# New places in memory for the split weights and the split activations of a float32r decoder trunk

## The chip, the cores and the metric

The kernel runs on one core of a Trainium2 chip. Its time is device time in microseconds (us); two runs of the kernel before gave 2322.8 and 2322.99 us, median 2322.89 us. One more execution was recorded by the hardware profiler, and every row quoted below comes from such a recording.

The core has several engines with instruction queues of their own. PE (TensorE) multiplies matrices; the profile shows its weight loads as a row of their own, PEld, because they run beside the multiplication. DVE (VectorE) and ACT (ScalarE) work elementwise, POOL (GpSimd) does a little copying, and SP (SyncE) issues the weight transfers from HBM.

## The reference

A two-layer decoder trunk over 272 tokens (16 learned meta tokens and 256 input tokens), model width 2048, 16 heads of 128, feed-forward width 8192, all in float32:

```
h = concat(meta, x)                                   # 272 x 2048
a = rms_norm(h);  q,k,v,f = a @ fox_w_in              # layer 0
h += forgetting_attention(q, k, v, cumsum(log_sigmoid(f + b))) @ fox_w_o
h += square(relu(rms_norm(h) @ w_up[0])) @ w_down[0]
c = rms_norm(h);  K,V = c @ w_kv                      # shared K/V
h += stick_breaking_attention(rms_norm(h) @ sb_w_q, K, V) @ sb_w_o   # layer 1
h += square(relu(rms_norm(h) @ w_up[1])) @ w_down[1]
return rms_norm(h)[16:]
```

The weight products are nearly all of the work. Layer 0 and the shared K/V need all 272 tokens; from the query projection of layer 1 on, only the last 256 tokens are needed.

## The kernel before, in words

**Split numbers.** Each float32 operand of a large product is split into a high part (the number rounded to float32r, the reduced format that PE takes in one pass) and a low part (the rest). Of the four partial products three are kept: high weight times high activation, high weight times low activation, low weight times high activation. ACT writes the high parts (line 217 for weights, line 134 for activations), DVE writes the low parts (lines 218 and 135). Activations that come out of attention are split by `put_split` (line 358), and those of the feed-forward layer at lines 503 and 504.

**Groups.** `gemm_group` (line 182) computes 512 output features, in four accumulators `acc` of 128 features each (index m). It goes through 2048 input features in four blocks (kb) of four chunks of 128 (kc). A weight block is brought in by SP in two transfers of 512 KB (line 204), and each half is split into a tile `whi` and a tile `wlo` (lines 209 and 210). A half holds two chunks, so a tile is 2 x 512 numbers per partition. There are four buffers for each of `raw`, `whi` and `wlo`. The groups are numbered by a counter u from 1 to 96, in this order: 1 to 12 the projections of layer 0 (q, k, v for four heads at a time, attention work between them), 13 to 16 its output projection, 17 to 48 its feed-forward layer (four rounds of four up groups and four down groups), 49 to 52 the queries of layer 1, 53 to 60 the shared K and V with the attention of layer 1 between them, 61 to 64 the output projection, 65 to 96 the feed-forward layer of layer 1.

**Two forms of the inner loop.** A group over 272 tokens issues, for each chunk and each m, three matmuls with 272 moving columns (lines 247 to 249), 192 in a group. A group over 256 tokens is "paired": the high and the low part of a row of activations stand side by side, so that one matmul with 512 moving columns multiplies the high weight with both (line 237), and a second one with 256 columns multiplies the low weight with the high part (line 241); that is 64 matmuls of either kind in a group. The two halves of the accumulator are added up when it is emptied (lines 254 and 258). Group 96 takes its last accumulator in the form of three. Every matmul loads its own weights.

**Places.** A tile of split activations has room for 16 rows of 640 numbers and 64 more. `ROWS` (line 28) gives, for 272 tokens, a row pitch of 640 numbers, the high part at number 48 and the low part at 368; for 256 tokens a pitch of 576, the high part at 16 and the low part at 272. In the allocated program the tiles `whi`, `wlo` and `x` all start at multiples of 256 bytes. So, counted in bytes past a multiple of 256, weights start at 0 (a chunk is 2048 bytes and a block of 128 features 512 bytes); activation rows for 272 tokens start at 192, high and low alike, and those for 256 tokens at 64, high and low alike.

**What sets the order.** The Python order of the calls, arranged by the tile framework's own scheduler, fixes each engine's instruction order; within the groups the matmuls are tied to their written order (line 174). PE takes its instructions in that order.

**Other float32r matmuls.** The forget-gate products (lines 305 and 306) multiply the same activation rows of 272 with weight tiles that are 32 features wide; those tiles start at 32 and at 160 bytes past a multiple of 256. In the attention of layer 1, lines 600 to 605 multiply tiles of two runs of 256 or 144 columns, whose first number stands 224 bytes past a multiple of 256, with weights at 32.

Of the kernel before, what the change touches and what calls it, by code (L numbers as in the profile page):

```python
# [10 lines left out]
F32R = mybir.dt.float32r  # L11
# [4 lines left out]
P = 128  # L16
D = 2048
NC = D // P
M = 16
# [4 lines left out]
QSCALE = 1.0 / math.sqrt(P)  # L24
N_FF = 4


ROWS = {0: (640, 48, 368), M: (576, 16, 272)}
XROW = 640

G_A0, G_M0, G_KV, G_A1, G_M1, G_FIN = range(6)
# [3 lines left out]
def yoco_kernel(ctx: ExitStack, tc: tile.TileContext, hT_in, gains, b_f, w_f, w_qkv0, w_o0, w_up, w_dn,  # L35
# [7 lines left out]
    wspl = ctx.enter_context(tc.tile_pool(name="wspl", bufs=4))  # L43
# [75 lines left out]
    class Split:  # L119


        def __init__(self, label, t0):
            n = T - t0
            self.t0 = t0
            rows = xs.tile([P, NC * XROW + 64], F32R, tag="x", name=f"x_{label}")
            pitch, hi, lo = ROWS[t0]
            rows = rows[:, hi:hi + NC * pitch].rearrange("p (c t) -> p c t", c=NC)
            self.hi, self.lo = rows[:, :, :n], rows[:, :, lo - hi:lo - hi + n]
            self.both = rows[:, :, :2 * n]

    def split_chunk(sp, gi, c):

# [41 lines left out]
    def gemm_matmul(*args, **kw):  # L174

        ins = nc.tensor.matmul(*args, **kw).ins  # L176
        if queued and pinned[0]:
            tc.add_manual_dep(ins, queued[0].name, mybir.DependencyInfo(mybir.DependencyClass.NoSync,
                                                                        mybir.DependencyReason.DATA))
        queued[:] = [ins]  # L180

    def gemm_group(wblk, sp, t0, evac, before={}, after={}, load_x=None, pairs=False, apart=()):

        uid[0] += 1
        u = uid[0]
        accs = [pacc.tile([P, 512], F32, tag="acc", name=f"acc_{u}_{m}") for m in range(4)]  # L190
        n = T - t0
        for kb in range(4):
            src_w = wblk[kb].rearrange("p (k c) -> p k c", k=4)
            if kb in before:
                before[kb]()
            piece = 1 if load_x is not None and kb < 2 else 2
            raws = [wraw.tile([P, 2, 512], F32, tag="raw", name=f"raw_{u}_{kb}_{hf}") for hf in range(2)]
            for k0 in range(0, 4, piece):
                if load_x is not None:
                    load_x(range(4 * kb + k0, 4 * kb + k0 + piece))  # L200
                if load_x is not None and kb == k0 == 0:

                    for c0 in (0, 256):
                        nc.scalar.dma_start(raws[0][:, 0, c0:c0 + 256], src_w[:, 0, c0:c0 + 256])
                else:
                    nc.sync.dma_start(raws[k0 // 2][:, k0 % 2:k0 % 2 + piece], src_w[:, k0:k0 + piece])
            parts = []
            for hf in range(2):
                whi = wspl.tile([P, 2, 512], F32R, tag="whi", name=f"whi_{u}_{kb}_{hf}")
                wlo = wspl.tile([P, 2, 512], F32R, tag="wlo", name=f"wlo_{u}_{kb}_{hf}")  # L210
                boxes = [(o, piece, 0, 512) for o in range(0, 2, piece)]
                if load_x is not None and kb == hf == 0:
                    boxes[:1] = [(0, 1, 0, 256), (0, 1, 256, 512)]
                for o, no, c0, c1 in boxes:
                    src = raws[hf][:, o:o + no, c0:c1]
                    hp, lp = whi[:, o:o + no, c0:c1], wlo[:, o:o + no, c0:c1]
                    on_act = nc.scalar.activation(hp, src, AF.Copy)  # L217
                    on_dve = nc.vector.tensor_tensor(out=lp, in0=src, in1=hp.bitcast(F32), op=ALU.subtract)  # L218
                parts.append((whi, wlo))
            if kb in after:  # L220
                with tc.issue_after(on_act.ins), tc.issue_after(on_dve.ins):
                    after[kb]()


            if load_x is not None and kb == 0:
                runs = [([kc], range(4)) for kc in range(4)]
            elif kb in (0, 3):
                runs = [(range(4), [m]) for m in range(4)]
            else:
                runs = [(range(2 * hf, 2 * hf + 2), range(4)) for hf in range(2)]  # L230
            pinned[0] = load_x is None
            for kcs, ms in runs:
                paired = [m for m in ms if pairs and m not in apart]
                single = [m for m in ms if m not in paired]
                for kc in kcs:
                    for m in paired:
                        gemm_matmul(accs[m], parts[kc // 2][0][:, kc % 2, m * P:(m + 1) * P], sp.both[:, 4 * kb + kc],
                                    start=kb == kc == 0, stop=False)
                for kc in kcs:
                    for m in paired:  # L240
                        gemm_matmul(accs[m][:, :n], parts[kc // 2][1][:, kc % 2, m * P:(m + 1) * P],
                                    sp.hi[:, 4 * kb + kc], start=False, stop=kb == kc == 3)
                for m in single:
                    for kc in kcs:
                        wh, wl = (w[:, kc % 2, m * P:(m + 1) * P] for w in parts[kc // 2])
                        hi, lo = sp.hi[:, 4 * kb + kc], sp.lo[:, 4 * kb + kc]
                        gemm_matmul(accs[m][:, :n], wh, hi, start=kb == kc == 0, stop=False)
                        gemm_matmul(accs[m][:, :n], wh, lo, start=False, stop=False)
                        gemm_matmul(accs[m][:, :n], wl, hi, start=False, stop=kb == kc == 3)
                if kb == 3:  # L250
                    for m in ms:
                        evac(m, [accs[m][:, :n]] + ([accs[m][:, n:]] if m in paired else []))
# [18 lines left out]
    def load_x(chunks):  # L271
        c0, n = chunks[0], len(chunks)
        nc.sync.dma_start(hT[:, c0:c0 + n, :], hT_in[:, c0:c0 + n, :])
        if c0 == 0:
            nc.sync.dma_start(g_sb, gains)
        for c in chunks:
            split_chunk(xa, G_A0, c)
# [86 lines left out]
    for g in range(4):  # L364
# [11 lines left out]
        if g == 0:  # L376

            gemm_group(w_qkv0[0], xa, 0, lambda m, acc, qT=qT: nc.scalar.copy(qT[:, m, :], acc[0]),
                       after={kb: (lambda kb=kb: first_norm(kb)) for kb in range(4)}, load_x=load_x)
            gate_products()  # L380
            box["rstd"] = norm.finish()
            for m in range(4):
                evac_q(m, [qT[:, m, :]])
            forget_gates(box["rstd"])
        else:
            gemm_group(w_qkv0[3 * g], xa, 0, evac_q)
# [4 lines left out]
        def decays(j):  # L391

            for i, (o, n) in enumerate(((0, 144), (144, T))):
                nc.vector.scalar_tensor_tensor(out=s[:, j, o:o + n], in0=fk[:, j, :n],
                                               scalar=fq_sb[:, i, 4 * g + j:4 * g + j + 1],
                                               in1=maskA[:, o:o + n], op0=ALU.subtract, op1=ALU.add)

        gemm_group(w_qkv0[3 * g + 1], xa, 0, lambda m, acc: evac_kv(m, acc, kT),
                   after={j: (lambda j=j: decays(j)) for j in range(4)})

# [255 lines left out]
    a, y, t, rs = (fin[:, i, :] for i in range(4))  # L656
# [81 lines left out]
```

## Time and profile before

| what | value |
|---|---|
| median of two runs | 2322.89 us |
| profiled execution | 2323.63 us |
| span of its instructions | 2321.9 us |
| PE busy | 2310.8 us (100%) |
| PEld busy | 2190.4 us (94%) |
| DVE busy | 1350.6 us (58%) |
| ACT busy | 1064.0 us (46%) |
| mean granted TensorE clock | 0.998 |

The span runs from the first to the last instruction; the profiled execution is 1.7 us longer than that. Matmuls are pipelined: the duration of one matmul in the profile (some 287 ns for 272 columns) overlaps with the next ones, so the price of a matmul is the distance from its start to the start of the next, which is read from a stretch of known length with a known count of matmuls in it, or from the start times in a timeline.

### The profile page before, as it was taken

What the parts mean: (1) busy time and instruction counts of PE and PEld (TensorE: products, weight loads), DVE (VectorE), ACT (ScalarE), POOL (GpSimd) and SP (SyncE); (2) the same over time, 40 slices, a digit from 0 to 9 for tenths busy, and PEclk for the clock granted to TensorE, in tenths of its full rate; (3) what the DMA queues carried; (4) which work ended last, traced back from release to release, by engine and by line L of the source; (5) the groups of instructions that cost most, each with busy time, mean ns of one, the idle gap of its engine ahead of it and who ended that gap; (6) DMA issues with size and microseconds to landing.
All of it is one profiled execution on the core that took longest, in us unless ns stands there. A gap on an engine that the chain in (4) does not pass through costs nothing.

```text
span 2321.9 us, 39954 instructions
## 1 busy us (share of the span) xinstructions
PE 2310.8 (100%) x16486; PEld 2190.4 (94%) x16486; DVE 1350.6 (58%) x1923; ACT 1064.0 (46%) x1477; POOL 39.9 (2%) x58
## 2 busy tenths in 40 slices
PE   9999999999999999999999999999999999999998
PEld 9999999999999999999998999988888888888887
DVE  7665555655455455445566655567665665665665
ACT  6434344544344344344455444455544543543553
POOL 1000000000000000000000000000000000000000
PEclk9999999999999999999999999999999999999999
DMA  6544444455555455555556444455555555556553
GB/s 233 172 156 165 171 158 173 171 183 173 183 175 183 171 186 176 178 182 171 187 173 200 155 145 146 146 175 186 197 184 193 192 186 198 186 184 199 181 199 127
DMA packets 116630, 412.00 MB, mean 177 GB/s; under 512 B 13264, under 2 KB 16736, under 8 KB 116448
## 3 DMA queue, kind: packets, MB, share of 16 engines
q1 hardware_dynamic: 114560, 406.29, 51.4%
q10 hardware_dynamic: 1888, 3.16, 0.4%
q8 instruction: 129, 2.11, 0.4%
q14 instruction: 53, 0.43, 0.1%
HBM read 407.29 MB, written 2.11 MB: 176 GB/s over the span
## 4 chain that ended last, share of the span: by engine, by line
PE 99%; DMA 0%; DVE 0%; ACT 0%; issue 0%; DVEq 0%; SPq 0%; ACTq 0%
PE acc L176 95%; PE ps L406 0%; PE pza L585 0%; PE pv L339 0%; PE po L468 0%; PE po L624 0%; DMA raw<-w_qkv 0%; PE po L625 0%; PE pzb L586 0%; PE po L469 0%; DMA hT<-hT_in 0%; PE po L626 0%; DVE ob L680 0%; PE pf L306 0%; PE pf L305 0%; PE pta L600 0%
## 5 line engine op out<-in xcount | busy, mean ns | idle before, releaser
L218 DVE TENSOR_TENSOR wlo<-raw,whi 128x1024 fp32r<-128x1024 f32 (+1 forms) x773 | 931.5, 1217 | 746.8 <-ACT whi L217 745.2
L217 ACT ACTIVATE whi<-raw 128x1024 fp32r<-128x1024 f32 (+1 forms) x773 | 799.2, 1050 | 953.9 <-PE acc L176 877.4
L176 PE MATMUL acc<-x_u,whi 128*128 128x272 f32 (+2 forms) x3088 | 647.5, 321 | 0.0
L176 PE MATMUL acc<-x_m,whi 128*128 128x272 f32 (+1 forms) x3072 | 646.1, 322 | 0.0
L176 PEld LDWEIGHTS acc<-x_u,whi 128*128 128x128 f32 x3088 | 499.9, 188 | 26.7
L176 PEld LDWEIGHTS acc<-x_m,whi 128*128 128x128 f32 x3072 | 497.8, 188 | 27.4
L176 PE MATMUL acc<-x_u,wlo 128*128 128x272 f32 (+1 forms) x2048 | 445.9, 282 | 0.0
L176 PE MATMUL acc<-x_m,wlo 128*128 128x272 f32 (+1 forms) x2048 | 443.7, 282 | 0.0
L176 PE MATMUL acc<-x_a,whi 128*128 128x272 f32 (+1 forms) x1792 | 360.6, 306 | 0.4 <-ACT x_a L134 0.2
L176 PEld LDWEIGHTS acc<-x_u,wlo 128*128 128x128 f32 x2048 | 340.3, 188 | 15.7
L176 PEld LDWEIGHTS acc<-x_m,wlo 128*128 128x128 f32 x2048 | 339.5, 188 | 15.9
L176 PEld LDWEIGHTS acc<-x_a,whi 128*128 128x128 f32 x1792 | 284.4, 188 | 9.9 <-issue 0.7
L176 PE MATMUL acc<-x_a,wlo 128*128 128x272 f32 (+1 forms) x1024 | 254.5, 286 | 0.0
L176 PE MATMUL acc<-x_kv,whi 128*128 128x272 f32 x1024 | 194.1, 288 | 0.0
L176 PEld LDWEIGHTS acc<-x_a,wlo 128*128 128x128 f32 x1024 | 179.6, 188 | 4.9 <-issue 0.5
L176 PE MATMUL acc<-x_o,whi 128*128 128x272 f32 (+1 forms) x768 | 162.3, 322 | 0.0
L176 PEld LDWEIGHTS acc<-x_kv,whi 128*128 128x128 f32 x1024 | 160.6, 188 | 0.4
L176 PE MATMUL acc<-x_kv,wlo 128*128 128x272 f32 x512 | 147.3, 288 | 0.0
L256 DVE TENSOR_TENSOR hT<-acc,hT 128x256 f32<-128x256 f32 (+1 forms) x239 | 102.4, 428 | 71.4 <-PE acc L176 69.5
L176 PEld LDWEIGHTS acc<-x_o,whi 128*128 128x128 f32 x768 | 124.3, 188 | 6.8
L176 PE MATMUL acc<-x_o,wlo 128*128 128x272 f32 (+1 forms) x512 | 111.6, 283 | 0.0
L176 PEld LDWEIGHTS acc<-x_kv,wlo 128*128 128x128 f32 x512 | 96.5, 188 | 0.1
(226 smaller groups left out, 1040.0 us busy)
## 6 DMA issues: line engine op xcount, KB each, us to landing
raw<-w_up SPq DMA_DIRECT2D x256, 512.0 KB, 4.7
raw<-w_dn SPq DMA_DIRECT2D x256, 512.0 KB, 4.7
raw<-w_qkv SPq DMA_DIRECT2D x92, 512.0 KB, 3.8
raw<-w_o SPq DMA_DIRECT2D x64, 512.0 KB, 4.5
raw<-w_kv SPq DMA_DIRECT2D x64, 512.0 KB, 3.6
raw<-w_q SPq DMA_DIRECT2D x32, 512.0 KB, 4.6
fk<-f_dram ACTq DMA_DIRECT2D x4, 544.0 KB, 5.0
raw<-w_qkv SPq DMA_DIRECT2D x7, 256.0 KB, 4.8
```

Of the source, the lines that this page charges most:

```text
L176: ins = nc.tensor.matmul(*args, **kw).ins
L217: on_act = nc.scalar.activation(hp, src, AF.Copy)
L218: on_dve = nc.vector.tensor_tensor(out=lp, in0=src, in1=hp.bitcast(F32), op=ALU.subtract)
L256: nc.vector.tensor_tensor(out=hT[:, c, t0:], in0=a, in1=hT[:, c, t0:], op=ALU.add)
```

## The change

The tiles `whi` and `wlo` are allocated 64 numbers wider per chunk (pitch 576 instead of 512 numbers) and used from a first column that a new function gives, separately for the high and for the low weights, by the group's number u: 0, 16, 32 or 48 numbers, which is 0, 64, 128 or 192 bytes. In the up groups of both feed-forward layers the 16 combinations of high and low displacement occur once each; in the down groups the high displacement is 16 or 0 numbers and the low one goes through all four.

The rows of activations have a pitch of 640 numbers in every stage, and each stage has a place for the high and for the low part. In most stages the two parts now stand at different bytes past a multiple of 256: 192 and 0 (`a0`), 0 and 192 (`kv`, `u1_3`), 192 and 64 (`o0`), 0 and 64 (`a1`), 64 and 128 (`o1`), 192 and 0 (`m1`), 128 and 192 (`u1_2`). In the others both stand alike: 192 (`m0`, as before), 224, 240, 160 and 0 (`u0_0` to `u0_3`), 64 and 0 (`u1_0`, `u1_1`).

In paired groups the matmul with 512 columns now reads two runs of 256 columns a given distance apart, 304 numbers in five stages; in `u1_0` and `u1_1` the distance is 256 and the two runs touch, as before. Where the low part stands first in the row, the products of high activations land in the second half of the accumulator, and the matmul of the low weight adds there.

The instructions on every engine and their order are the same as before; the splitting of a full half of weights now writes two runs of 512 numbers instead of one of 1024.

```diff
-ROWS = {0: (640, 48, 368), M: (576, 16, 272)}
+ROWS = {"a0": (48, 384), "kv": (0, 304), "o0": (48, 336), "m0": (48, 368), "u0_0": (56, 376),
+        "u0_1": (60, 380), "u0_2": (40, 360), "u0_3": (0, 320),
+        "a1": (320, 16), "o1": (336, 32), "m1": (304, 0), "u1_0": (16, 272), "u1_1": (0, 256),
+        "u1_2": (352, 48), "u1_3": (0, 304)}
+
+
+def columns_of_weights(u):
+
+    quarter = (0, 16, 32, 48)
+    if u <= 16 or 53 <= u <= 60:
+        return quarter[u % 4], quarter[u % 4]
+    if 49 <= u <= 52 or 61 <= u <= 64:
+        return ((0, 0), (0, 32), (32, 0), (16, 16))[u % 4]
+    f, g = divmod((u - 17) % 48, 8)
+    if g < 4:
+        return quarter[f], quarter[g]
+    return (16 if u < 37 else 0), quarter[g - 4]
...
-            pitch, hi, lo = ROWS[t0]
-            rows = rows[:, hi:hi + NC * pitch].rearrange("p (c t) -> p c t", c=NC)
-            self.hi, self.lo = rows[:, :, :n], rows[:, :, lo - hi:lo - hi + n]
-            self.both = rows[:, :, :2 * n]
+            hi, lo = ROWS[label]
+            o = min(hi, lo)
+            rows = rows[:, o:o + NC * XROW].rearrange("p (c t) -> p c t", c=NC)
+            self.hi, self.lo = (rows[:, :, k - o:k - o + n] for k in (hi, lo))
+
+            d = abs(lo - hi)
+            if t0:
+                self.both = rows[:, :, :2 * d].rearrange("p c (i t) -> p c i t", i=2)[:, :, :, :n]
+            self.low_first = lo < hi
...
-                whi = wspl.tile([P, 2, 512], F32R, tag="whi", name=f"whi_{u}_{kb}_{hf}")
-                wlo = wspl.tile([P, 2, 512], F32R, tag="wlo", name=f"wlo_{u}_{kb}_{hf}")
+                whi, wlo = (wspl.tile([P, 2, 576], F32R, tag=f"w{x}", name=f"w{x}_{u}_{kb}_{hf}")[:, :, o:o + 512]
+                            for x, o in zip(("hi", "lo"), columns_of_weights(u)))
...
-                        gemm_matmul(accs[m][:, :n], parts[kc // 2][1][:, kc % 2, m * P:(m + 1) * P],
+                        gemm_matmul(accs[m][:, n:] if sp.low_first else accs[m][:, :n],
+                                    parts[kc // 2][1][:, kc % 2, m * P:(m + 1) * P],
```

## The prediction

> **What bounds the kernel now.** I read the first page of the profile first (busy shares, the chain that ended last), then the stretches of one stage each with the matmuls of line 176 alone, then the timeline of PE for single start times.
>
> ```profile
> span 2321.9 us, 39954 instructions
> PE 2310.8 (100%) x16486; PEld 2190.4 (94%) x16486; DVE 1350.6 (58%) x1923; ACT 1064.0 (46%) x1477; POOL 39.9 (2%) x58
> PE 99%; DMA 0%; DVE 0%; ACT 0%; issue 0%; DVEq 0%; SPq 0%; ACTq 0%
> core 0: 2321.9 us, clock 0.998
> ```
>
> The chain of work that ended last is PE for 99% of the span, at a granted clock of 0.998. PE has practically no idle time, so only two things can change the time: how many matmuls there are, and how far apart they start. To price a matmul I take two stretches in which nothing but group matmuls run, four groups each: down groups over 272 tokens, then down groups over 256 tokens (columns: stretch, its length, PE busy and count, PEld busy and count, granted clock, DMA).
>
> ```profile
> core 0: us, PE busy (x) PEld busy (x), PEclk, DMA share, GB/s
> 525.20:619.90 94.70, 94.70 (x770) 94.70 (x769) 1.00 0.53 178
> 1687.60:1776.10 88.50, 88.50 (x513) 77.72 (x512) 1.00 0.58 190
> ```
>
> Four groups over 272 tokens are 4 x 192 = 768 matmuls (the other two of the 770 belong to the neighbours): 94.70 us / 768 = **123.3 ns** each. Four paired groups are 256 pairs of a 512-column and a 256-column matmul: 88.50 us / 256 = **345.7 ns** a pair. The kernel has 56 groups of the first form and 40 of the second: 56 x 192 x 123.3 ns = 1326 us and 40 x 64 x 345.7 ns = 885 us, together 2211 us, 95% of the span. The other 111 us are attention, norms and the two ends, which the change does not touch.
>
> Is there room in these prices that could hang on a place in memory? The timeline of PE in a paired group says so (columns: start, length, engine and line, operation, count; a row begins where the one before it has issued its last matmul).
>
> ```profile
> 1709.74 1.09 PE L176 MATMUL acc<-x_u,whi 128*128 128x512 f32 x4
> 1710.67 0.62 PE L176 MATMUL acc<-x_u,wlo 128*128 128x256 f32 x4
> 1711.12 1.07 PE L176 MATMUL acc<-x_u,whi 128*128 128x512 f32 x4
> 1712.03 0.63 PE L176 MATMUL acc<-x_u,wlo 128*128 128x256 f32 x4
> 1712.50 0.40 PE L176 MATMUL acc<-x_u,whi 128*128 128x512 f32 x1
> ```
>
> Four matmuls with 512 columns take 0.93 and 0.91 us (230 ns each). Four with 256 columns take 0.45 us the first time and 0.47 us the second: 112.5 and 117.5 ns for the same shape, the same bytes past a multiple of 256 and a full clock. So there are two paces, and before any place is changed the kernel falls into both by turns.
>
> **The change part by part.** No instruction is added, removed or moved on any engine, and no wait; the transfers are the same. What changes is where PE reads, and where ACT and DVE write.
>
> *Matmuls over 272 tokens (10752).* Only group 17 keeps all its places. What another place costs, the trace shows at one spot with the same activation rows (192 past a multiple of 256) and weights at 32 and 160, in tiles 32 features wide: the gate products.
>
> ```profile
> 31.69 0.29 PE L306 MATMUL pf<-x_a,wf 128*32 128x272 f32 x1
> 31.82 0.28 PE L305 MATMUL pf<-x_a,wf 128*32 128x272 f32 x1
> ...
> 32.69 0.29 PE L306 MATMUL pf<-x_a,wf 128*32 128x272 f32 x1
> 32.81 0.29 PE L305 MATMUL pf<-x_a,wf 128*32 128x272 f32 x1
> ```
>
> Eight matmuls lie between the two rows of either line: 1.00 and 0.99 us, 124.4 ns each, 1.1 ns more than 123.3. The lower bound is the faster of the two paces above, carried over by columns: 112.5 x 272 / 256 = 119.5 ns, 3.8 less. The upper bound is the slowest float32r row of the trace, where the moving tile starts 224 past a multiple of 256:
>
> ```profile
> 1320.53 0.40 PE L600 MATMUL pta<-eh,ntri_r 128*128 128x512 f32 x1
> 1320.77 0.29 PE L604 MATMUL ptb<-eh,ntri_r 128*128 128x288 f32 x1
> ...
> 1322.50 0.39 PE L601 MATMUL pta<-el,ntri_r 128*128 128x512 f32 x1
> 1322.73 0.30 PE L602 MATMUL pta<-eh,nones_r 128*128 128x288 f32 x1
> 1322.86 0.30 PE L603 MATMUL pta<-el,nones_r 128*128 128x288 f32 x1
> 1323.00 0.30 PE L605 MATMUL ptb<-el,ntri_r 128*128 128x288 f32 x1
> ```
>
> Two matmuls with 288 columns take 0.27 us, 135 ns each; by columns 127.5 ns for 272, 4.2 more. I take the gate products' 1.1 ns, the nearest row in shape: 10560 x 1.1 ns = **+12 us**, between -41 and +45 us.
>
> *Matmuls with 512 columns in two runs.* In `a1`, `o1`, `m1`, `u1_2` and `u1_3`, 32 groups, they read two runs that no longer touch: 2032 matmuls. Lines 600 and 601 read two runs of 256: 0.24 and 0.23 us, 235 ns, against 230 in one run. The timeline rounds to 10 ns, so the 5 ns are an upper figure; the mean durations in the groups (next fence) differ by 2 to 3 ns. I take 2.5 ns: **+5 us**, between 0 and +10.
>
> ```profile
> L176 PE MATMUL acc<-x_m,whi 128*128 128x512 f32 x1024 | 266.8, 393 | 0.0
> L176 PE MATMUL acc<-x_u,whi 128*128 128x512 f32 x1008 | 262.6, 392 | 0.0
> L600 PE MATMUL pta<-eh,ntri_r 128*128 128x512 f32 x8 | 3.2, 395 | 0.0
> ```
>
> *Matmuls over 256 tokens otherwise (2560 pairs).* Other places may shift how often each pace occurs. With the fast pace throughout, a pair costs 3 x 112.5 = 337.5 ns, 8.2 less, -21 us; with 240 for 512 columns (the slower of the two rows above) and 117.5 for 256 it costs 357.5 ns, 11.8 more, +30 us, which holds the runs of the paragraph before. Nothing says which way it shifts: 0.
>
> *Splitting the weights in two runs of 512.* The trace before has no such write; its cost lies between nothing and twice the present one.
>
> ```profile
> L218 DVE TENSOR_TENSOR wlo<-raw,whi 128x1024 fp32r<-128x1024 f32 (+1 forms) x773 | 931.5, 1217 | 746.8 <-ACT whi L217 745.2
> L217 ACT ACTIVATE whi<-raw 128x1024 fp32r<-128x1024 f32 (+1 forms) x773 | 799.2, 1050 | 953.9 <-PE acc L176 877.4
> 5.50:331.00 325.50, 325.35 (x2566) 319.14 (x2567) 200.46 (x387) 143.61 (x238) 20.59 (x22) 1.00 0.51 177
> 430.00:1188.20 758.20, 758.20 (x6148) 758.12 (x6148) 396.76 (x484) 326.93 (x419) 0.00 (x0) 1.00 0.52 178
> ```
>
> The last two rows are stretches with all engines: PE, PEld, DVE, ACT, POOL. ACT's idle time before line 217 ended 877.4 us long on PE, which had to free a buffer: the split runs ahead of PE. Doubled, DVE's 8 x 1.217 = 9.7 us a group would add 32 x 9.7 = 312 us to 397 in the feed-forward stretch of 758, and 12 x 9.7 = 117 to 200 in the first stretch of 325.5: still under PE, in the latter barely. I cost it at nothing; PE hides it. ACT, at 8 x 1.05 us a group, stays further below.
>
> **Sum:** 12 + 5 = +17 us on a span of 2321.9, 2339 us; the profiled execution is 1.7 us longer than its span (2323.63 us) and 0.7 over the median of the runs (2322.89), so **2340 us**, 0.7% slower. About 2% is what a measurement can tell from no change, so this counts as no change.
>
> **The rivals.** *Places cost nothing* (chance 0.12): every stage keeps 123.3 and 345.7 ns, 2323 us. For it: five rows of different shapes and places lie within a few per cent per column. Against it: the 0.45 and 0.47 us above show a sensitivity to something. The Trainium skill, "TensorE: Matmul & The Clock Gate", section "Step-by-step: what each phase is for", states this rival as a rule: the streamed operand and the weight load have read ports of their own, so loading the next weights takes nothing from the running matmul. By that rule displacing the weights would leave the time at 2323 us. The trace agrees in so far as 32-wide weights don't make a 272-column matmul cheaper than 128-wide ones (124.4 against 123.3 ns); no run so far displaces the weights alone.
>
> *The new places hold PE in the fast pace* (faster, the other side). If the two paces come from how the streamed row and the weights being loaded meet, unlike places can keep them apart everywhere. Price: -41 - 21 = -62 us, 2261 us. It decides when at least three quarters of the matmuls go at 112.5 ns per 256 columns; then the gain passes 46 us, 2%. Against it: the 96 groups get many different combinations, and one that helps is followed by three that need not. Full effect 0.04; part of it, ending between 2277 and 2323 us, 0.20.
>
> *The new places bring them together* (slower by over 2%). PEld is busy for 94% of the span, so a weight load goes beside nearly every matmul; where both run over the same places, a matmul waits. Price at the slow rows: +45 + 30 = +75 us, 2399 us. It decides from 46 / 2211 = 2.1% on the mean group: 125.9 ns for 272 columns, 353 ns a pair. For it: every float32r row with other places is dearer per column than the groups. Against it: none reaches 4%, and the displacements run through all quarters. Chance 0.14.
>
> **How the numbers follow.** The forecast case, a little slower, ending between 2323 and 2369 us, has 0.50. Faster by over 2%: 0.04; within 2%: 0.50 + 0.12 + 0.20 = 0.82; slower by over 2%: 0.14. The range 2300 to 2385 us leaves out the full gain and the lowest quarter of the partial one (0.09), and the upper half of the slow case (0.07). The outer bounds, 2261 and 2399 us, would need all 96 groups to lie at one end.
>
> **What the profile after would show.** Groups 17 and 69 keep all their places: 23.7 and 22.1 us each, as now (94.70 / 4, 88.50 / 4). The groups over 272 tokens should stand between 23 and 24.5 us, differing from group to group as their displacements differ; if all stand at 23.7, places cost nothing. Paired groups in two runs should be slower than 69 to 72 by some 64 x 2.5 ns = 0.16 us. DVE and ACT may be busier, but PE must not wait for `whi` or `wlo`; if it does, the cover was too thin. The forecast is wrong if the groups differ by over 5%, or if all shift the same way.

## The result and the profile after

The changed kernel takes **2350.84 us** (median of two runs, 2350.51 to 2351.17) against 2322.89 us: ratio 1.0119, 95% interval 1.0101 to 1.0138. That is 28 us slower, less than the 2% within which a result counts as no change here, and clear of the measurement's own spread. The forecast was 2340 us, the range 2300 to 2385.

The page of the changed kernel: span, busy shares and, from the chain that ended last, the shares by engine.

```profile
span 2349.4 us, 39954 instructions
PE 2337.8 (100%) x16486; PEld 2213.8 (94%) x16486; DVE 1350.8 (57%) x1923; ACT 1064.8 (45%) x1477; POOL 40.2 (2%) x58
PE 99%; DMA 1%; DVE 0%; ACT 0%; issue 0%; SPq 0%; DVEq 0%; ACTq 0%
```

The count of instructions is the same, DVE and ACT are as busy as before within a microsecond (1350.6 and 1064.0 us before), and PE is 27.0 us busier. Nearly all of the loss, 27.0 of 27.5 us of span, is in the pace of PE.

Where it lies is read from the stretches from the first matmul of a stage to the first of the next (columns in all such fences: stretch, its length, busy time and count of PE, PEld, DVE, ACT and POOL, granted clock, DMA share, GB/s). First the kernel before: groups 1 to 12, 13 to 16, 17 to 48, 49 to 52, 53 to 60, 61 to 64 and 65 to 95.

```profile
5.49:331.00 325.51, 325.36 (x2566) 319.15 (x2567) 200.47 (x387) 143.62 (x238) 20.60 (x22) 1.00 0.51 177
331.00:430.06 99.06, 99.06 (x803) 98.85 (x801) 56.50 (x78) 47.03 (x67) 2.57 (x3) 1.00 0.50 171
430.06:1188.28 758.22, 758.22 (x6148) 758.14 (x6147) 396.76 (x484) 326.95 (x419) 0.00 (x0) 1.00 0.52 178
1188.28:1277.43 89.15, 89.15 (x516) 78.28 (x515) 60.81 (x88) 47.14 (x70) 0.00 (x0) 1.00 0.57 189
1277.43:1504.06 226.63, 226.63 (x1755) 221.42 (x1754) 128.97 (x182) 108.26 (x136) 8.16 (x7) 1.00 0.43 149
1504.06:1598.46 94.40, 94.40 (x550) 82.91 (x548) 62.15 (x95) 47.16 (x67) 1.17 (x1) 1.00 0.53 179
1598.46:2286.07 687.61, 687.61 (x3972) 603.93 (x3971) 425.53 (x579) 332.11 (x467) 0.00 (x0) 1.00 0.57 190
```

The same stages of the changed kernel:

```profile
5.26:335.24 329.98, 329.04 (x2568) 323.00 (x2567) 200.68 (x386) 143.52 (x238) 21.18 (x24) 1.00 0.52 175
335.24:435.41 100.17, 100.17 (x802) 99.96 (x801) 56.58 (x78) 46.98 (x67) 2.57 (x3) 1.00 0.51 169
435.41:1206.06 770.65, 770.65 (x6148) 770.57 (x6147) 396.52 (x484) 327.61 (x419) 0.00 (x0) 1.00 0.53 175
1206.06:1296.23 90.17, 90.17 (x516) 78.89 (x515) 60.96 (x88) 47.16 (x70) 0.00 (x0) 1.00 0.57 187
1296.23:1525.52 229.29, 229.29 (x1756) 224.04 (x1755) 129.02 (x182) 108.47 (x136) 8.16 (x7) 1.00 0.44 147
1525.52:1620.38 94.86, 94.86 (x549) 82.96 (x548) 62.08 (x95) 47.11 (x67) 1.17 (x1) 1.00 0.54 178
1620.38:2313.45 693.07, 693.07 (x3973) 606.62 (x3971) 425.70 (x579) 332.27 (x467) 0.00 (x0) 1.00 0.58 189
```

Every stage lost, 0.9 to 2.0 ns a matmul. The stages over 272 tokens lost 4.5 + 1.1 + 12.4 + 2.7 = 20.7 us, those over 256 tokens 1.0 + 0.5 + 5.5 = 7.0 us; the granted clock is 1.00 in all of them. Of the 4.5 us of the first stage 0.8 are not pace: PE stands idle there for 329.98 - 329.04 = 0.94 us, against 0.15 before.

Within a stage the loss isn't even. First two groups of the kernel before, 18 and 94, from the first matmul to the first of the next group:

```profile
454.20:477.88 23.68, 23.68 (x194) 23.68 (x193) 12.76 (x16) 11.34 (x17) 0.00 (x0) 1.00 0.52 178
2241.74:2263.90 22.16, 22.16 (x130) 19.46 (x129) 14.07 (x20) 11.60 (x17) 0.00 (x0) 1.00 0.59 190
```

Single groups of the changed kernel: 18, 22, 26, then 69, 94 and 80.

```profile
459.56:483.88 24.32, 24.32 (x195) 24.32 (x194) 12.76 (x16) 11.43 (x17) 0.00 (x0) 1.00 0.52 173
555.76:579.45 23.69, 23.69 (x195) 23.69 (x193) 11.21 (x12) 8.26 (x9) 0.00 (x0) 1.00 0.51 178
651.89:676.20 24.31, 24.31 (x194) 24.31 (x193) 12.74 (x16) 11.38 (x17) 0.00 (x0) 1.00 0.52 174
1710.11:1732.26 22.15, 22.15 (x131) 19.47 (x129) 13.93 (x20) 10.39 (x15) 0.00 (x0) 1.00 0.58 189
2269.03:2291.00 21.97, 21.97 (x131) 19.28 (x129) 14.05 (x20) 11.59 (x17) 0.00 (x0) 1.00 0.60 191
1955.79:1978.32 22.53, 22.53 (x130) 19.56 (x129) 12.84 (x16) 8.26 (x9) 0.00 (x0) 1.00 0.55 187
```

In group 18 only the low weights moved, by 64 bytes, and it takes 24.32 instead of 23.7 us. Group 22 has its rows at 224 and both weights at 64, places that differ from before throughout, and takes the 23.7 us of before. Group 26 (rows 192, both weights 64) takes 24.31. Group 69, which keeps its places, takes 22.15 as before; group 94 is faster than that, group 80 slower. The places alone don't sort these groups, but the distance between row and weights may: 192 - 0 = 192 bytes in the kernel before and 224 - 64 = 160 in group 22 go at the old pace, 192 - 64 = 128 in group 26 at a slow one. From this came the theory that the experiments test: **the pace of PE depends on the distance, modulo 256 bytes, between the row it streams and the weights**, not on the place of either.

### The profile page after: what moved, and what is told of

Its sections match the earlier page's. It is cut to its first block, busy times and chain, and to the rows that moved or that the text cites. A ratio compares the mean times of both kernels' runs of the same rounds, so it can differ in the third digit from the quotient of the medians.

```text
span 2349.4 us, 39954 instructions
## 1 busy us (share of the span) xinstructions
PE 2337.8 (100%) x16486; PEld 2213.8 (94%) x16486; DVE 1350.8 (57%) x1923; ACT 1064.8 (45%) x1477; POOL 40.2 (2%) x58
## 4 chain that ended last, share of the span: by engine, by line
PE 99%; DMA 1%; DVE 0%; ACT 0%; issue 0%; SPq 0%; DVEq 0%; ACTq 0%
PE acc L198 95%; DMA hT<-hT_in 0%; PE ps L429 0%; PE pza L608 0%; PE pv L362 0%; PE po L491 0%; PE po L647 0%; PE pzb L609 0%; PE po L648 0%; PE po L492 0%; DMA g_sb<-gains 0%; PE po L649 0%; DVE ob L703 0%; PE pf L329 0%; PE pf L328 0%; PE pta L623 0%
## 5 line engine op out<-in xcount | busy, mean ns | idle before, releaser
L198 PE MATMUL acc<-x_m,whi 128*128 128x272 f32 (+1 forms) x3072 | 655.6, 324 | 0.0
```

## The experiments

In the code below `...` stands for lines left out.

**Everything moved together.** All rows and all weights start 64 bytes later than in the kernel before, with the wider weight tiles and the row pitch of the changed kernel.

```diff
-ROWS = {0: (640, 48, 368), M: (576, 16, 272)}
+ROWS = dict.fromkeys(("a0", "kv", "o0", "m0", "u0_0", "u0_1", "u0_2", "u0_3"), (64, 384)) | dict.fromkeys(("a1", "o1", "m1", "u1_0", "u1_1", "u1_2", "u1_3"), (32, 288))
...
+def columns_of_weights(u):
+    return 16, 16
```

> Everything of the kernel before moved by the same 64 bytes: weights at 64 past a multiple of 256 (in the wider tiles), activation rows over 272 tokens at 0, over 256 tokens at 128, high and low alike. Theory (the distance between the streamed row and the weights, modulo 256 bytes, decides): nothing changes, 2323 us within 2 us, groups over 272 tokens at 23.7 us. Rival 1 (the row's own place decides, whatever the weights'): the rows over 272 tokens stand at 0 as in groups 45 to 48 of the changed kernel, 0.38 us a group dearer, 56 x 0.38 = +21 us, 2344 us. Rival 2 (the wider pitch of the weight tiles or their splitting in two runs costs by itself): over 2325 us with all groups shifted alike.

Measured: 2323.43 us against 2323.56, ratio 0.9999 (0.9990 to 1.0009). Groups 21 to 24 and 69 to 72, first in the kernel before, then in this run:

```profile
525.25:619.97 94.72, 94.72 (x771) 94.72 (x770) 45.58 (x50) 34.30 (x36) 0.00 (x0) 1.00 0.53 178
1687.57:1776.24 88.67, 88.67 (x515) 77.89 (x513) 52.43 (x68) 35.21 (x39) 0.00 (x0) 1.00 0.58 190
525.08:619.80 94.72, 94.72 (x771) 94.72 (x769) 45.60 (x50) 34.30 (x36) 0.00 (x0) 1.00 0.52 178
1687.34:1776.01 88.67, 88.67 (x515) 77.88 (x513) 52.47 (x68) 35.23 (x39) 0.00 (x0) 1.00 0.58 190
```

The paces are those of before to a hundredth. Both rivals fall: a place by itself costs nothing, and neither do the wider tiles and the splitting in two runs, which this kernel has too. In the wider tiles the second chunk lies 2304 bytes behind the first instead of 2048, so half of the weights have moved against their rows by 256 bytes more, and that changed nothing either.

**The weights alone.** The changed kernel with the rows of the kernel before.

```diff
-ROWS = {"a0": (48, 384), "kv": (0, 304), "o0": (48, 336), "m0": (48, 368), "u0_0": (56, 376),
...
+ROWS = dict.fromkeys(("a0", "kv", "o0", "m0", "u0_0", "u0_1", "u0_2", "u0_3"), (48, 368)) | dict.fromkeys(("a1", "o1", "m1", "u1_0", "u1_1", "u1_2", "u1_3"), (16, 272))
```

> The displaced weights alone, with the rows of the kernel before (192 and 64 past a multiple of 256). Theory (distance decides): the displacements are most of the loss. Groups 1 to 48 and 53 to 60 by the prices of the same distances in the changed kernel: +25 us; the 40 paired groups some 0.2 us each, +8 us; together 2323 + 33 = 2356 us, more than the whole change. Rival 1 (weight loads have a port of their own and their place is indifferent): 2323 us, every group as before. Rival 2 (the costs of the two edits add up and are of like size): 2337 us.

Measured: 2353.14 us, ratio 1.0127 (1.0112 to 1.0142): 29.6 us, more than the whole change, as the theory had it (33). Displacing nothing but the weights slows matmuls whose streamed rows have not moved.

**The rows alone.** The changed kernel with weights at 0 in tiles of 512 numbers per chunk.

```diff
-    return (16 if u < 37 else 0), quarter[g - 4]
+    return 0, 0
...
-                whi, wlo = (wspl.tile([P, 2, 576], F32R, tag=f"w{x}", name=f"w{x}_{u}_{kb}_{hf}")[:, :, o:o + 512]
+                whi, wlo = (wspl.tile([P, 2, 512], F32R, tag=f"w{x}", name=f"w{x}_{u}_{kb}_{hf}")[:, :, o:o + 512]
```

> The rows of the changed kernel alone, weights back at 0 in tiles of 512. Theory (distance decides): each stage costs what the changed kernel's groups with weights at 0 cost: +9 us over 272 tokens, +5 us over 256 tokens, 2337 us. Rival 1 (weights indifferent, rows alone decide): the whole change, 2351 us. Rival 2 (rows indifferent): 2323 us. The two-run matmuls of my prediction would show as paired stages dearer than u1_0 by at least 0.16 us a group.

Measured: 2339.84 us, ratio 1.0071 (1.0056 to 1.0086): 16.3 us; the theory said 14, both rivals fall. Weights alone and rows alone add up to 46 us, the change with both costs 28: where both move, the distances are others again, and some come back to where they were. Four groups each, all with both parts of the row alike: 25 to 28 (row at 192), 21 to 24 (224), 29 to 32 (240) and 37 to 40 (160).

```profile
625.21:719.93 94.72, 94.72 (x770) 94.72 (x769) 50.31 (x62) 44.12 (x62) 0.00 (x0) 1.00 0.52 178
527.94:625.21 97.27, 97.27 (x771) 97.27 (x769) 45.59 (x50) 34.37 (x36) 0.00 (x0) 1.00 0.51 174
719.93:815.93 96.00, 96.00 (x770) 96.00 (x769) 45.59 (x50) 34.34 (x36) 0.00 (x0) 1.00 0.51 176
910.66:1005.40 94.74, 94.74 (x770) 94.74 (x769) 45.60 (x50) 34.35 (x36) 0.00 (x0) 1.00 0.52 178
```

Rows at 224 take 97.27 us with weights at 0; in the changed kernel group 22, with weights at 64, had them at the old pace.

That the low part stands first in the row, and the matmul of the low weight adds into the second half of the accumulator, need not cost anything. Groups 62 and 63 have it in this run and take 22.08 us each, less than the 22.17 of a paired group before:

```profile
1544.13:1588.30 44.17, 44.17 (x259) 38.53 (x258) 30.73 (x49) 22.67 (x33) 0.00 (x0) 1.00 0.56 191
```

**All distances.** Rows as before, both weights displaced alike, 16 bytes further from group to group.

```diff
...
+def columns_of_weights(u):
+    o = 4 * ((u - 1) % 16)
+    return o, o
```

> Rows as before, high and low weights displaced alike by 0, 16, 32 ... 240 bytes, one step a group, so that groups 17 to 32, 33 to 48, 65 to 80 and 81 to 96 each go through all 16 distances. Theory (distance decides): the steps of 64 bytes repeat the changed kernel's groups (23.56 us from first to last matmul start at 0, 24.19 at 64 and 128, 23.94 at 192), the steps between lie between them, and both sweeps over 272 tokens agree to 0.05 us. Rival (the pace is an accident of the moment at which a group begins, since the kernel before shows two paces for the same places): the two sweeps disagree by up to 0.5 us at the same distance. Time some 2340 us either way.

Measured: one run, 2358.66 us, some 19 us more than I expected. The two sweeps over 272 tokens agree to 0.01 us, the two over 256 tokens too (groups 17, 65 and 96, at the ends of their stages, left aside): with high and low weights displaced alike, the pace is no accident of the moment. Groups 33, 35, 37, 38, 41, 43 and 45, with weights at 0, 32, 64, 80, 128, 160 and 192:

```profile
823.18:846.87 23.69, 23.69 (x195) 23.69 (x194) 12.00 (x14) 10.09 (x14) 0.00 (x0) 1.00 0.52 178
871.18:894.86 23.68, 23.68 (x195) 23.68 (x193) 12.73 (x16) 11.33 (x17) 0.00 (x0) 1.00 0.53 178
919.18:943.50 24.32, 24.32 (x195) 24.32 (x193) 11.94 (x14) 9.51 (x12) 0.00 (x0) 1.00 0.51 173
943.50:967.18 23.68, 23.68 (x194) 23.68 (x193) 11.21 (x12) 8.25 (x9) 0.00 (x0) 1.00 0.53 178
1015.82:1040.14 24.32, 24.32 (x195) 24.32 (x193) 12.01 (x14) 10.15 (x14) 0.00 (x0) 1.00 0.51 173
1064.28:1088.42 24.14, 24.14 (x194) 24.14 (x193) 12.75 (x16) 11.41 (x17) 0.00 (x0) 1.00 0.51 174
1112.43:1136.50 24.07, 24.07 (x195) 24.07 (x193) 13.18 (x17) 11.15 (x16) 0.00 (x0) 1.00 0.51 175
```

So a matmul with 272 columns costs 23.69 / 192 = 123.4 ns at the best and 24.32 / 192 = 126.7 ns at the worst distance. The steps of 64 bytes repeat the changed kernel's prices. My guess for the steps between failed: they don't lie between their neighbours (weights at 80 go at the best pace, with the worst at 64 and 128 on both sides), and most of them are dear, which made the run longer than I expected. The distance rule fails once there, too: weights at 16 against rows at 192 (group 34, below) are slow, while group 30 of the changed kernel, with weights at 64 and rows at 240, has the same distance of 176 bytes and takes 23.68 us. Below 64 bytes something besides the distance counts, which stays open.

```profile
846.87:871.18 24.31, 24.31 (x195) 24.31 (x193) 12.77 (x16) 11.43 (x17) 0.00 (x0) 1.00 0.52 175
```

Nor do the distances always settle a single pace. Group 42 has the same places in the changed kernel and in the run with the weights alone (rows at 192, high weights at 192, low weights at 64), and takes 24.21 us in the one and 23.90 in the other:

```profile
1037.21:1061.42 24.21, 24.21 (x194) 24.21 (x193) 12.72 (x16) 11.38 (x17) 0.00 (x0) 1.00 0.54 173
1040.14:1064.04 23.90, 23.90 (x195) 23.90 (x193) 12.73 (x16) 11.37 (x17) 0.00 (x0) 1.00 0.51 176
```

Over 256 tokens the two are closer: in the run with everything moved, groups 50 to 52 take 22.09 us and groups 62 to 64, with the same places, 22.17. What picks between two such paces stays open. For the rule speaks the rest of the traces: three distances belong to a group (high row to high weights, low row to high weights, high row to low weights), and in groups 14 to 16, 18 to 48 and 53 of all the kernels profiled here 13 such sets occur at two or more different places. In 11 of them the times from first to last matmul agree to 0.06 us; the other two are the set of group 42 and the distance of 176 bytes.

**Two runs alone.** With the places of the kernel before, in the wider weight tiles, the low row over 256 tokens stands 320 numbers after the high one (pitch 640, as in the change).

```diff
-ROWS = {0: (640, 48, 368), M: (576, 16, 272)}
+ROWS = dict.fromkeys(("a0", "kv", "o0", "m0", "u0_0", "u0_1", "u0_2", "u0_3"), (48, 368)) | dict.fromkeys(("a1", "o1", "m1", "u1_0", "u1_1", "u1_2", "u1_3"), (16, 336))
...
+def columns_of_weights(u):
+    return 0, 0
```

> The kernel before with one edit: in all rows over 256 tokens the low part stands 320 instead of 256 numbers after the high part, so both still start 64 bytes past a multiple of 256, but the 512-column matmul reads two runs that don't touch. The prediction's term (two runs cost 2.5 ns): 2544 x 2.5 ns = +6 us, 2329 us, paired groups at 22.3 us instead of 22.1. Theory (distances modulo 256 bytes alone decide, two runs cost nothing): no change, 2323 us.

Measured: 2323.16 us, ratio 0.9999 (0.9989 to 1.0009). Groups 69 to 72:

```profile
1688.60:1777.27 88.67, 88.67 (x514) 77.88 (x513) 52.47 (x68) 35.21 (x39) 0.00 (x0) 1.00 0.57 190
```

Nothing: reading two runs costs nothing where the distances stay, and my term falls.

**No writes, no transfers.** Both weights displaced by 64 bytes in the feed-forward groups; in half of these PE multiplies the tiles of the first block again instead of those of the other three, for which nothing is loaded or split. The kernel computes another result.

```diff
+    return (16, 16) if 17 <= u <= 48 or u >= 65 else (0, 0)
...
+            quiet = kb > 0 and (25 <= u <= 32 or 41 <= u <= 48 or 73 <= u <= 80 or 89 <= u <= 96)
...
-            for k0 in range(0, 4, piece):
+            for k0 in range(0, 0 if quiet else 4, piece):
...
+            if not quiet:
+                parts = []
+            for hf in range(0 if quiet else 2):
```

> Rows as before, both weights displaced by 64 bytes in groups 17 to 48 and 65 to 96. In groups 25 to 32, 41 to 48, 73 to 80 and 89 to 96 the weights of blocks 1 to 3 are left out: no transfer and no split, PE multiplies the tiles of block 0 again, so the result is another one and DVE, ACT and the DMA rest there, while PE issues the same matmuls. Theory (the streamed row meets PE's own weight loads): the quiet groups go as slowly as the loud ones, 24.2 us from first to last matmul start over 272 tokens and 22.3 over 256. Rival (the rows and weights read by PE meet the writes of ACT and DVE or the transfers, which were displaced with them): the quiet groups fall to 23.6 us or less and to 22.1 us or less, some 10 us for the whole kernel.

Measured: one run, 2352.01 us. Loud groups 21 to 24 and quiet groups 25 to 28, then loud 69 to 72 and quiet 73 to 76:

```profile
527.47:624.75 97.28, 97.28 (x770) 97.28 (x769) 45.56 (x50) 34.31 (x36) 0.00 (x0) 1.00 0.50 174
624.75:722.03 97.28, 97.28 (x770) 97.28 (x769) 21.09 (x38) 19.27 (x38) 0.00 (x0) 1.00 0.13 44
1708.64:1798.24 89.60, 89.60 (x515) 78.61 (x513) 52.45 (x68) 35.16 (x39) 0.00 (x0) 1.00 0.55 188
1798.24:1887.84 89.60, 89.60 (x515) 78.62 (x513) 26.86 (x53) 22.56 (x51) 0.00 (x0) 1.00 0.14 48
```

DVE halves, the transfers fall from 174 to 44 GB/s, and the pace does not move by a hundredth. In the quiet group 32 there is a stretch of 72 matmuls in which DVE, ACT, POOL and the transfers do nothing at all:

```profile
805.51:814.63 9.12, 9.12 (x75) 9.12 (x74) 0.00 (x0) 0.00 (x0) 0.00 (x0) 1.00 0.00 0
```

9.12 us / 72 = 126.7 ns, the full price. The writes of ACT and DVE and the transfers have no part in it; only PE's own matmuls and weight loads are left.

**A search.** Unlike places of high and low rows, nearly all in combinations that no run had.

```diff
+ROWS = dict.fromkeys(("a0", "o0"), (0, 288)) | {"m0": (0, 304), "kv": (48, 368)}
+ROWS |= dict.fromkeys(("u0_0", "u0_1", "u0_2", "u0_3"), (0, 336))
+ROWS |= {"a1": (16, 272), "o1": (16, 272), "m1": (0, 304)}
+ROWS |= dict.fromkeys(("u1_0", "u1_1", "u1_2", "u1_3"), (0, 288))
...
+    f, g = divmod((u - 17) % 48, 8)
+    return quarter[f], quarter[g % 4]
```

> A search over distances that no run had: over 272 tokens the low row stands 192 (m0), 64 (u0_0 to u0_3) or 128 bytes (a0, o0) past the place of the high row, over 256 tokens 192 (m1) or 128 (u1_0 to u1_3), each with the 16 displacements of high and low weights. Theory: group 66 has the distances of group 94 of the changed kernel (high row 0, low row 192, high weights 0, low weights 64) and takes as long, 21.86 us from first to last matmul start, 0.19 less than before. Over 272 tokens I expect no group under 23.56 us, since none of the 32 combinations so far was; if one is, a version that beats both kernels can be made of it. Rival (the place of a tile in the whole memory counts too): group 66 differs from 21.86 by over 0.1 us.

Measured: one run, 2348.79 us. Group 66, with the distances of group 94 of the changed kernel, takes as long as that one (21.97 us to the first matmul of the next group):

```profile
1639.61:1661.58 21.97, 21.97 (x130) 19.29 (x129) 14.16 (x21) 12.31 (x21) 0.00 (x0) 1.00 0.57 191
```

The places are those of group 94 too, and only the stage, the tile and the moment are others, so this shows that the price carries over; that the distances alone carry it is shown where the places differ, by the run with everything moved and the sets above. Over 272 tokens the best of the new combinations took 23.71 us, so none beat the old pace.

**The best distances everywhere.** Over 256 tokens the distances of group 94, over 272 tokens those of before.

```diff
+ROWS = dict.fromkeys(("a0", "kv", "o0", "m0", "u0_0", "u0_1", "u0_2", "u0_3"), (48, 368)) | dict.fromkeys(("a1", "o1", "m1", "u1_0", "u1_1", "u1_2", "u1_3"), (0, 304))
+def columns_of_weights(u):
+    return (0, 16) if 49 <= u <= 52 or u >= 61 else (0, 0)
```

> A version made of the best distances found: over 272 tokens everything as before (rows at 192, weights at 0), over 256 tokens the high row at 0, the low row at 192, high weights at 0, low weights at 64. Theory: 39 paired groups take 21.86 instead of 22.05 us from first to last matmul start, 39 x 0.19 = 7.4 us, group 96 unknown; 2323 - 7 = 2316 us, ratio 0.997. Rival (what a place costs in one group doesn't hold when all groups use it): 2323 us or more.

Measured: **2316.18 us** against 2323.52, ratio 0.9970 (0.9959 to 0.9981), 7.3 us faster than before and so faster than both kernels, by less than the 2% but clear of the spread. Groups 69 to 72, and PE's timeline in one of them (columns: start, length, engine and line, operation, count):

```profile
1684.33:1772.22 87.89, 87.89 (x514) 77.14 (x513) 52.33 (x68) 35.21 (x39) 0.00 (x0) 1.00 0.57 191
...
1709.97 0.62 PE L187 MATMUL acc<-x_u,wlo 128*128 128x256 f32 x4
1710.42 1.08 PE L187 MATMUL acc<-x_u,whi 128*128 128x512 f32 x4
1711.34 0.62 PE L187 MATMUL acc<-x_u,wlo 128*128 128x256 f32 x4
1711.79 1.54 PE L187 MATMUL acc<-x_u,whi 128*128 128x512 f32 x6
```

Both runs of four 256-column matmuls now take 0.45 us. The kernel before took 0.45 and 0.47 by turns: the gain is that the slower of its two paces is gone, while four with 512 columns still take 0.92 us.

**Finer places.** The best version with weights moved by 16 bytes a step.

```diff
+    if g < 4:
+        return 0, 4 * (4 * f + g)
+    if u <= 48:
+        return 4 * (4 * f + g - 4), 0
+    return (0, 16) if f == 3 else (4 * (4 * f + g - 4), 4 * (4 * f + g - 4) + 16)
```

> Around the best distances in steps of 16 bytes: in the up groups the low weights alone go through 0, 16, ... 240 bytes, over 272 and 256 tokens; in the down groups over 272 tokens the high weights alone; in 12 of the down groups over 256 tokens both weights together, the low ones 64 bytes further. Theory (distances in quarters of 256 bytes decide, other steps are mostly worse): no group over 272 tokens falls under 23.55 us, none over 256 tokens under 21.85. Rival (finer places matter on their own and a better one is left): some group falls clearly under these.

Measured: one run, 2340.16 us. No group beat its limit: the fastest are the controls, 23.7 us over 272 tokens, and 21.97 us over 256 tokens in group 93:

```profile
2236.77:2258.74 21.97, 21.97 (x130) 19.29 (x129) 14.17 (x21) 12.22 (x19) 0.00 (x0) 1.00 0.59 191
```

## Why the prediction was right, and where it wasn't

*PE sets the end, and only its pace can change the time*: right. PE's busy time grew by 27.0 us, the span by 27.5; the rest is the idle time in the first stage.

*Slower by 0.7%, within 2%*: right in sign and class; 17 us were forecast, 28 came. The terms were less right than their sum, and some luck is in it: 5 us for a cost that doesn't exist stood in for 7 us that had been put at nothing.

*Matmuls over 272 tokens, +12 us*: the mechanism was right, the size too small. "I take the gate products' 1.1 ns" is the step: 20.7 us over 10752 matmuls are 1.9 ns (without the 0.8 us of idle time 1.85). The sweep shows why one row couldn't give it: the price takes different values between 0 and 24.32 / 192 - 23.69 / 192 = 3.3 ns. The weights of the gate products stand at 32 and at 160 in turn; in the sweep these two places cost 0 and 24.14 / 192 - 23.68 / 192 = 2.4 ns, 1.2 in the mean. The 1.1 ns were probably the mean of two prices, though no run separates the gate products. The upper bound of 4.2 ns held. The lower one, 3.8 ns less, was never approached: no distance tried went under 123.3 ns, so the fast pace of 256 columns does not carry over to 272.

*Two runs, +5 us*: wrong. "I take 2.5 ns" read the difference between lines 600 and 176 as the price of the second run; with equal distances two runs cost nothing (ratio 0.9999). Lines 600 and 601 also have another place than the groups.

*Otherwise over 256 tokens, 0*: wrong by 7.0 us. "Nothing says which way it shifts" missed that the place of before was already one of the better ones, which the trace before could not show: in the sweep every other distance was dearer for these groups, and of the combinations in the changed kernel only a few, as in group 94, are cheaper. A walk over all of them loses.

*Splitting in two runs, nothing*: right. DVE stayed at 1350.8 us, and the run with everything moved together, which splits in the same way, took the time of before.

*The rival that places cost nothing* falls with the weights-alone run, +29.6 us. The Trainium skill, "TensorE: Matmul & The Clock Gate", section "Step-by-step: what each phase is for", has the two operands read through ports of their own, so that loading weights takes no read bandwidth from the running matmul. The measurement decides against what the rival drew from it for these float32r matmuls: moving nothing but the weights changed their pace by up to 3.3 ns in 123. Whether the ports have a part in that no run shows.

*The rival that unlike places keep PE in the fast pace* holds for single combinations over 256 tokens, and used everywhere it gives 7.3 us, not 62. *The rival that the places meet everywhere* was right that the place of the weights against that of the row counts, but not in how: equal places (distance 0, 24.07 us a group) are cheaper than distances of 64 and 128 (24.32). Its size was too large: even the worst distance of the sweep, 126.7 ns in all 10752 matmuls, is 3.3 x 10752 = 35 us.

*The signs*: groups 17 and 69 kept their time, though that of group 17 is 24.15 us before and after, not the 23.7 that I took from four other groups; groups over 272 tokens with no attention work in them lay between 23.7 and 24.3 us, differing with their displacements. That groups in two runs would stand above 69 to 72 by 0.16 us was wrong as a rule: group 94 stands below them, and group 80, whose runs touch, above. All groups shifting the same way was to be a sign against the forecast: over 272 tokens none got faster, over 256 tokens groups 64, 81, 83 and 94 did. That PE must not wait for `whi` held but for the first group, where it waited 0.9 us:

```profile
L198 PE MATMUL acc<-x_a,whi 128*128 128x272 f32 (+1 forms) x1792 | 364.7, 307 | 0.9 <-ACT whi L239 0.9
```

The run with the weights alone splits in the same way and has no idle time in that stage, so the cover was not too thin.

## What to carry to other kernels

When PE has no gap left, the place of its operands is still a quantity: look at the start-to-start distance of equal matmuls, not only at busy shares, and if it takes more than one value at full clock, try displacing the weights against the streamed rows. What counts here is, in the main, the distance between the two, so a best place found for one operand can be lost when the other moves; change both together, or search pairs. A kernel that gives every group another displacement measures many of them in one profile, and a best one found in a single group held when all groups used it.

## What was not expected of the hardware

The pace of float32r matmuls depends on the distance between the streamed row and the weights modulo 256 bytes: 123.4 to 126.7 ns for 272 columns in the sweep, 21.97 us for one paired group of the changed kernel and 22.53 for another. With high and low weights displaced alike it repeats to 0.01 us a group within the sweep, and it is the same when ACT, DVE and the DMA rest. Why the pace depends on this distance, what counts below 64 bytes, what picks between the two paces that one set of places can have (24.21 and 23.90 us), and why 272 columns never go under 123.3 ns stay open; no run here separates these.
